# A decoder layer in fp32 pieces: a quarter of the projection of p moved ahead of the first product, with changes of order at the entries and the end

## The chip, the cores and the metric

The kernel runs on one core of a Trainium2 chip. The metric is the device time of one execution in microseconds (us). The engines are TensorE (PE, matmuls; its weight loads are shown as PEld), VectorE (DVE), ScalarE (ACT), GpSimd (POOL) and SyncE (SP). Nearly all transfers are issued on SP's queue, some on POOL's.

## The reference

One layer over 1024 tokens of width 1024, in fp32. Cut to what matters here:

```python
x = x + 0.5 * swiglu(rms_norm(x, ffn1_norm), ffn1_w_gate, ffn1_w_up, ffn1_w_down)   # D_FF = 2816
h = rms_norm(x, mix_norm)
fq, fk, fv, f_logit, sq, sk, sv, g_fox, g_sb = split_columns(h @ w_in)
...                          # forgetting attention (8 heads) and stick-breaking attention (8 heads)
x = x + (sigmoid(g_fox) * (y_fox @ w_branch_fox) + sigmoid(g_sb) * (y_sb @ w_branch_sb)) @ w_out
x = x + 0.5 * swiglu(rms_norm(x, ffn2_norm), ffn2_w_gate, ffn2_w_up, ffn2_w_down)
x = x + sigmoid(rms_norm(x, ple_norm) @ w_ple_gate) * (p @ w_ple_proj)      # p: 1024 x 256
```

The last product, p @ w_ple_proj, depends on the inputs alone, so it can be computed at any place. It is a matrix of 1024 features by 1024 tokens with an inner size of 256.

## The kernel before

All products are fp32 by splitting: an operand is cast to a "high" half (fp32r), the rest is its "low" half, and high*high, high*low and low*high are accumulated. Casts are on ACT, the subtractions for low halves on DVE or POOL (`split`, L105 and L106). Features lie on partitions; a PSUM bank holds 128 features by 512 tokens.

The stages follow one another: FFN 1 (its front is `first_entry`), the mixer's gates and projections, attention, the output projection, FFN 2, and the last stage (`ple_start`), which computes sigmoid(...) * (p @ w_ple_proj) and stores the output. The large products are done in pairs of 128-column weight blocks by seven products instead of eight, numbered 1 to 7 (`make_up`; L617 is the matmul). `up_order` is the list of products (n, m): n is the pair, m the product. It is the same for FFN 1, the mixer's gates, FFN 2 and the last stage; its first ten steps are called an entry here. Products 1, 6, 7 and 4 of one n share a PSUM bank ("b"); the result after 6 is copied out by ACT before 7 adds into that bank. `begin(s)` does operand sums that belong to step s of the list.

The order on each engine is that in which the code is written in these stages (a manual schedule). A few instructions outside them are placed by the scheduler; one is the scaling of the small tile `gqk` (q_norm and k_norm, L1615 to L1617), used only in attention.

In `first_entry` the eight token tiles of x are loaded (512 KB each, L1527) with the first weights between them, the norm's gain is spread over all partitions by two matmuls (`spread`, L239), `busy(4)` runs four matmuls on zeros (L253), tokens are squared and scaled, turned by PE (L273), and cast (`rows_high`, L282) and subtracted (`rows_low`, L287) into the operands H. The first product is `F.plain(0, 0, ...)` (L561).

In attention the projection of p is done in 16 units (`p_units`): group d of 512 features, four blocks m, two token halves, six matmuls of 128x512 each (L1056). Each result is copied from PSUM to a tile and stored in `p_proj` (DRAM). Around them stand the stacks of query and key of the first head, and behind them the first scores (L1150, L1151), which need the bias tile GF, loaded from `forget_sums` (L1430) and added to the mask by POOL (L1142).

In the last stage the list `AT` says behind which step the `p_proj` tiles are fetched and the results finished. `finish` multiplies a gate tile by `p_proj` on DVE (L1716) and adds `x_end`: by an accumulating DMA on POOL's queue (L1719) followed by the output store on the same queue (L1722), or, for the last pieces, by a DVE addition (L1721) and a store on SP's queue.

Of the kernel before, what the change touches and what calls it, by code (L numbers as in the profile page):

```python
# [11 lines left out]
F32R = mybir.dt.float32r  # L12
BF16 = mybir.dt.bfloat16
AF = mybir.ActivationFunctionType
ALU = mybir.AluOpType
# [3 lines left out]
P = 128  # L19
# [17 lines left out]
def tile_hybrid_decoder_layer(  # L37
# [42 lines left out]
    def pe(ins):  # L80
        order("pe", ins)
# [163 lines left out]
    def busy(n):  # L245

        if not zero:
            zero.append(slot("T", [P, 512], BF16))
            nc.vector.memset(zero[0][:], 0.0)
            return  # L250
        ps = bank("av")
        for _ in range(n):
            pe(nc.tensor.matmul(ps[:], zero[0][:, 0:P], zero[0][:], start=True, stop=True))  # L253

    def rows_stat(N, t, tag, first=False):
        xt = N["x"][:, t, :]
# [27 lines left out]
    def rows_low(N, t):  # L284
        cs = slice(t * P, (t + 1) * P)
        for b, v in enumerate(N["v"].pop(t)):
            nc.vector.tensor_sub(N["B"][b][:, 1, :, cs], v, f(N["B"][b][:, 0, :, cs]))  # L287
# [741 lines left out]
    def p_units(d, pT, new_bank):  # L1029

        cell = {}
        add_load(cell, lambda: wload([kp(w_ple_proj[0])[:, :, d * 512:d * 512 + 512]], 2, 512))

        def fetch():
            weights(cell, 1)
            for k in range(2):
                pT[k] = slot("RAW", [P, S])
                nc.sync.dma_start(pT[k][:], p[0, 0, k * P:(k + 1) * P, :])
            return
            yield  # L1040

        def operand(k):
            if k == 0:
                pT["t"] = slot("X", [P, 2, 2, S], F32R)
            split(pT["t"][:, k, 0, :], pT["t"][:, k, 1, :], pT[k][:], nc.scalar, nc.vector)
            return
            yield

        def unit(t):
            w = weights(cell)  # L1050
            ps = new_bank()
            m, half = divmod(t, 2)
# [6 lines left out]
            if half == 0:  # L1059
# [3 lines left out]
            if half:  # L1063
# [458 lines left out]
    def first_entry(F):  # L1522
# [30 lines left out]
        F.prep(0, 1)  # L1553
        rows_high(N[0], 2, ps2)
# [148 lines left out]
    def ple_start():  # L1703
# [9 lines left out]
        def finish(n, i, h=slice(0, 2), cols=slice(0, 512), add_in_dma=True):  # L1713

            e = E[n][i][:, h, cols]
            nc.vector.tensor_mul(e, e, T[n, i][:, h, cols])  # L1716
            queue = nc.gpsimd if add_in_dma else nc.sync
            if add_in_dma:
                queue.dma_start(e, xe[2 * n + i].rearrange("p (h n) -> p h n", h=2)[:, h, cols], accum_op=ALU.add)  # L1719
            else:  # L1720
                nc.vector.tensor_add(e, e, T[n, i, "x"][:, h, cols])  # L1721
            queue.dma_start(out[0, (2 * n + i) * P:(2 * n + i + 1) * P, :].rearrange("p (h n) -> p h n", h=2)[:, h, cols], e)  # L1722
# [4 lines left out]

        def evict(n, m, ps):
            if m == 1:
                E[n] = [slot(t, [P, 2, 512]) for t in (("Y", "Y") if n == 2 else ("GF", "RN"))]  # L1730
            e1, e2 = E[n]
            if m == 1:
                nc.scalar.copy(e1[:, 0, :], ps[:])
# [18 lines left out]
        AT = {4: [(finish, 0, 0)], 5: [(fetch, 2, 1, "T")], 6: [(finish, 0, 1), (fetch, 1, 0, "Q"), (fetch, 1, 1, "Q"), (fetch, 3, 0, "KH"), (fetch, 3, 0, "KH", True)],  # L1752
              7: [(fetch, 3, 1, "T")], 9: [(finish, 1, 0)], 10: [(fetch, 3, 1, "Q", True)], 11: [(finish, 1, 1)], 12: [(fetch, 2, 0, "Q")],
              13: [(finish, 2, 1)], 14: [(finish, 3, 0, h0), (fetch, 2, 0, "T", True)], 16: [(finish, 3, 1, h1, *late)], 17: [(finish, 2, 0, slice(0, 2), *late), (finish, 3, 0, h1, *late)]}

        def begin(i, X):
            if not Xs:
# [56 lines left out]
```

## Time and profile before

| what | value |
|---|---|
| median of 3 runs | 2258.56 us (2258.21 to 2259.16) |
| the profiled execution, its own time | 2257.49 us |
| its span in the trace | 2255.8 us |
| PE busy | 2213.0 us (98%) |
| DVE, ACT, POOL busy | 1507.5, 1005.5, 823.3 us |
| granted clock of PE | 0.996 of full speed |
| DMA | 298.30 MB, mean 132 GB/s over the span |

A timeline row gives the start, the busy time, the engine, the line, the operation with its output and input tiles, how many, and in brackets the idle time before it with what ended that idle time. "SPq" and "POOLq" rows are transfers being issued; their landing is later. A row of the stretches (A:B) gives the busy time of PE, PEld, DVE, ACT and POOL with counts, then the clock, the DMA share and GB/s. A row of the DMA view gives tile, queue, count, size and microseconds from issue to landing.

### The profile page before, as it was taken

Reading aid. Unit: us, or ns where it says so; the run is one execution under the profiler, and the core shown is the slowest. Engines: PE = TensorE matmul, PEld = TensorE weight load, DVE = VectorE, ACT = ScalarE, POOL = GpSimd, SP = SyncE. Lnnn points to the kernel's source line nnn. Section 1 sums busy time; section 2 is a strip of 40 time slices with the busy share of each in tenths; the row PEclk is TensorE's granted clock in tenths of the full one; section 3 lists DMA queues with packets and bytes.
Section 4 is the critical chain, followed back from the end, with each engine's and each line's share of the span. In section 5 each row is a group of like instructions: output and inputs, shape, how many; then the busy total and the mean of one; then the engine's idle time right before and its main releaser. Section 6 shows DMA issues by size and latency. Waiting matters only on the chain. (4 is left out here: it accounts for less than half of the span.)

```text
span 2255.8 us, 30537 instructions
## 1 busy us (share of the span) xinstructions
PE 2213.0 (98%) x11210; PEld 1879.2 (83%) x11210; DVE 1507.5 (67%) x2365; ACT 1005.5 (45%) x1805; POOL 823.3 (36%) x794
## 2 busy tenths in 40 slices
PE   9999999999999999999999999999999999999996
PEld 7788888888888899999898888888888888888885
DVE  8755555588887325666678775799554545778895
ACT  6333333433455445555566663255333333433452
POOL 2344535200021336565567664411544444100211
PEclk9999999999999999999999999999999999999998
DMA  3332323394323333333323366641323232754427
GB/s 131 103 126 82 129 80 131 126 332 173 112 94 123 120 115 103 85 113 85 85 66 93 104 196 233 244 159 45 127 103 108 95 116 94 281 196 149 140 84 210
DMA packets 196263, 298.30 MB, mean 132 GB/s; under 512 B 28745, under 2 KB 108873, under 8 KB 196114
## 3 DMA queue, kind: packets, MB, share of 16 engines
q1 hardware_dynamic: 194448, 290.58, 39.1%
q0 software_dynamic: 1664, 5.77, 1.1%
q8 instruction: 88, 1.44, 0.3%
q14 instruction: 61, 0.50, 0.1%
q10 hardware_dynamic: 2, 0.00, 0.0%
HBM read 196.40 MB, written 83.13 MB: 124 GB/s over the span
## 5 line engine op out<-in xcount | busy, mean ns | idle before, releaser
L509 PE MATMUL ps<-H,H 128*128 128x512 f32 x2184 | 497.3, 389 | 0.0
L509 PEld LDWEIGHTS ps<-H,H 128*128 128x128 f32 x2184 | 409.5, 188 | 84.9
L617 PE MATMUL ps<-H,WL 128*128 128x512 f32 x1164 | 275.5, 389 | 0.7 <-ACT GF L1735 0.7
L617 PEld LDWEIGHTS ps<-H,WL 128*128 128x128 f32 x1164 | 218.4, 188 | 46.4 <-ACT GF L1735 1.1
L185 POOL TENSOR_TENSOR PT<-PT,PT 128x512 f32<-128x512 f32 x27 | 35.0, 1294 | 403.9 <-ACT PT L182 403.0
L617 PE MATMUL ps<-H,Q 128*128 128x512 f32 x624 | 148.4, 389 | 0.0
L517 DVE SCALAR_TENSOR_TENSOR X<-ps,X 128x512 f32<-128x512 f32 x168 | 110.3, 686 | 47.4 <-PE ps L509 47.3
L617 PE MATMUL ps<-X,WL 128*128 128x512 f32 (+1 forms) x588 | 138.9, 385 | 1.1 <-ACT Y L779 0.7
L617 PEld LDWEIGHTS ps<-H,Q 128*128 128x128 f32 x624 | 117.1, 188 | 24.3
L617 PE MATMUL ps<-H,PT 128*128 128x512 f32 x540 | 128.8, 389 | 0.0
L617 PEld LDWEIGHTS ps<-X,WL 128*128 128x128 f32 x588 | 108.8, 188 | 23.8 <-ACT Y L779 1.1
L139 POOL TENSOR_TENSOR WL<-RAW,WH 128x512 fp32r<-128x512 f32 (+1 forms) x84 | 97.4, 1181 | 67.3 <-ACT WH L129 43.2
L1217 DVE TENSOR_TENSOR PT<-ps,PT 128x512 fp32r<-128x512 f32 (+1 forms) x160 | 100.0, 627 | 31.0 <-ACT PT L1211 30.1
L617 PEld LDWEIGHTS ps<-H,PT 128*128 128x128 f32 x540 | 101.2, 188 | 21.3 <-ACT GF L1735 0.3
L894 PE MATMUL ps<-WH,H 128*128 128x256 f32 x768 | 116.1, 287 | 0.8 <-ACT RN L959 0.8
L902 PE MATMUL ps<-H,WH 128*128 128x512 f32 x384 | 115.0, 406 | 0.0
L1235 PE MATMUL ps<-PT,X 128*128 128x256 f32 (+1 forms) x640 | 102.7, 286 | 6.5 <-DVE PT L1217 5.5
L1211 ACT CAST PT<-ps 128x512 fp32r<-128x512 f32 (+1 forms) x160 | 87.1, 548 | 42.6 <-PE ps L1209 41.5
L1235 PEld LDWEIGHTS ps<-PT,X 128*128 128x128 f32 x640 | 90.3, 190 | 17.2 <-DVE PT L1217 10.4
L894 PEld LDWEIGHTS ps<-WH,H 128*128 128x128 f32 x768 | 101.4, 190 | 2.6 <-ACT RN L959 1.2
L412 POOL TENSOR_TENSOR PT<-GF,RN 128x512 f32<-128x512 f32 x20 | 33.6, 1682 | 190.8 <-DVE GF L802 190.8
L1163 POOL TENSOR_TENSOR T<-T,l 128x128 f32<-128x128 f32 (+3 forms) x64 | 73.2, 1148 | 71.9 <-DVE l L1162 69.7
(441 smaller groups left out, 4781.7 us busy)
## 6 DMA issues: line engine op xcount, KB each, us to landing
hidden<-PT SPq DMA_DIRECT2D x40, 512.0 KB, 2.6
WH<-in_ffn_w_gate_dram SPq DMA_DIRECT2D x38, 512.0 KB, 4.7
Q<-hidden SPq DMA_DIRECT2D x24, 512.0 KB, 6.0
hidden<-RN SPq DMA_DIRECT2D x22, 512.0 KB, 2.6
KH<-in_ffn_w_up_dram SPq DMA_DIRECT2D x20, 512.0 KB, 6.2
KL<-in_ffn_w_up_dram SPq DMA_DIRECT2D x20, 512.0 KB, 6.9
T<-in_ffn_w_down_dram SPq DMA_DIRECT2D x20, 512.0 KB, 6.5
GF<-hidden SPq DMA_DIRECT2D x14, 512.0 KB, 7.7
```

The costliest lines, as they stand in the source:

```text
L139: ins = eng_lo.tensor_sub(lo[part], raw[part], f(hi[part]))
L185: add = lambda eng: eng.tensor_add(N["acc"], N["acc"], d)
L412: eng.tensor_add(s12[:, 0, :], g1[:, 1, :], g2[:, 1, :])
L509: pe(nc.tensor.matmul(groups[g][t][:], wt[:, b, k, t * P:(t + 1) * P], act[:, a, k, :], start=(fresh and n == 0), stop=(i in (6, 1, 4) and ...
L517: nc.vector.scalar_tensor_tensor(xs, groups[g][t][:], scale, xs, ALU.mult, ALU.add)
L617: pe(nc.tensor.matmul(ps[:, cols], hl[:, a, k, :], right(B[m], b, k)[:, cols], start=(first and i == 0), stop=(final and i == 11), skip_gr ...
L894: pe(nc.tensor.matmul(ps[:, :n], hT[t // 4](a, k)[:, (t % 4) * P:(t % 4 + 1) * P], w[k // 4][b][:, k % 4, :n], start=(i == 0), stop=(i == ...
L902: pe(nc.tensor.matmul(ps[:], w[a][:, k, :], hT[half](b, k), start=(i == 0), stop=(i == 23)))
L1163: nc.gpsimd.tensor_mul(T[:, :n], T[:, :n], l[:].broadcast_to([P, n]))
L1211: high = nc.scalar.copy(pt[:, 0, :width], ps[:, :width])
L1217: ins = nc.vector.tensor_sub(pt[:, 1, :width], ps[:, :width], f(pt[:, 0, :width]))
L1235: pe(nc.tensor.matmul(o, lh, r, start=(kpair == c and i == 0), stop=(kpair == 0 and i == 3)))
```

## The change

- In the front, `p_begin` loads the first 512 tokens of p and the first 512 columns of w_ple_proj ahead of x. `p_split` makes their halves. Four products (`p_product`) of 128 features by 512 tokens stand between the turnings of the token tiles, and `p_out` copies and stores them. In attention, group 0 keeps only the second token half (four units instead of eight); it still loads and splits all of p.
- `busy(4)` goes, and `busy(6)` stands ahead of the spreading of the gain.
- In `up_order`, (2, 6) and (1, 7) change places; in `begin`, the operands of product 7 are made in step 1 instead of step 0.
- In the last stage all output stores go to SP's queue, the stores of accumulated tiles as separate steps (`store`), the half tile (3, 0) is finished by a DVE addition, and fetches, finishes and tiles are placed anew (`AT`).

The diff, cut to its core:

```diff
+    def p_begin():
+        raw = slot("Q", [P, 2, 512])
+        nc.sync.dma_start(raw[:], kp(p[0, 0])[:, :, 0:512])
+        wr = slot("RAW", [P, 2, 512])
+        nc.sync.dma_start(wr[:], kp(w_ple_proj[0])[:, :, 0:512])
+        return raw, wr
+    def p_split(raw, wr):
+        r = []
+        for src, tags in ((raw, ("KH", "KL")), (wr, ("RN", "GF"))):
+            hi, lo = (slot(t, [P, 2, 512], F32R) for t in tags)
+            split(hi[:], lo[:], src[:], nc.scalar, nc.vector)
+            r.append((hi, lo))
+        return r
+    def p_product(ops, m, ps):
+        n = 0
+        for a, b in ((0, 0), (1, 0), (0, 1)):
+            for k in range(2):
+                pe(nc.tensor.matmul(ps[:], ops[1][b][:, k, m * P:(m + 1) * P], ops[0][a][:, k, :], start=(n == 0), stop=(n == 5)))
+                n += 1
+        return ps
+    def p_out(m, ps):
+        o = slot("T", [P, 512])
+        nc.scalar.copy(o[:], ps[:])
+        nc.sync.dma_start(pd[m][:, 0:512], o[:])
...
-        seqn = [(2, 1), (1, 5), (2, 2), (1, 6), (1, 7), (2, 6), (2, 5), (1, 3), (2, 7), (1, 4)]
+        seqn = [(2, 1), (1, 5), (2, 2), (1, 6), (2, 6), (1, 7), (2, 5), (1, 3), (2, 7), (1, 4)]
...
             if s == 0:
                 sums(2, nc.vector, True)
+            elif s == 1:
                 for q in range(4):
                     combo_s(q, 7)
...
-        units = [(6 * 0.216, unit(t)) for t in range(NT)]
+        units = [(6 * 0.216, unit(t)) for t in range(d == 0, NT, 1 + (d == 0))]
...
+        p_raw = p_begin()
         load_x(0)
...
         busy(0)
+        busy(6)
         spread(N[0]["g"])
...
+        p_ops = p_split(*p_raw)
         for t in range(4):
             rows_stat(N[0], t, ("PT", "WL", "WL", "PT")[t], True)
             rows_mul(N[0], t)
-        busy(4)
+        pu = [p_product(p_ops, m, bank("sc")) for m in range(2)]
+        p_out(0, pu[0])
         rows_high(N[0], 0, ps1)
+        p_out(1, pu[1])
+        pu.append(p_product(p_ops, 2, bank("sc")))
         rows_high(N[0], 1, ps1)
...
         rows_low(N[0], 2)
+        p_out(3, p_product(p_ops, 3, ps2()))
...
-            queue = nc.gpsimd if add_in_dma else nc.sync
             if add_in_dma:
-                queue.dma_start(e, xe[...], accum_op=ALU.add)
+                nc.gpsimd.dma_start(e, xe[...], accum_op=ALU.add)
             else:
                 nc.vector.tensor_add(e, e, T[n, i, "x"][:, h, cols])
-            queue.dma_start(out[...], e)
+                store(n, i, h, cols)
+        def store(n, i, h=slice(0, 2), cols=slice(0, 512)):
+            nc.sync.dma_start(out[...], E[n][i][:, h, cols])
...
-        AT = {4: [(finish, 0, 0)], 5: [(fetch, 2, 1, "T")], 6: [(finish, 0, 1), ...
+        AT = {6: [(fetch, 1, 0, "Q"), (fetch, 1, 1, "WH")], 7: [(finish, 0, 0)], 8: [(finish, 0, 1), ...
```

What this does to the order on the engines, at three places. The names of semaphores in brackets say which engine or which transfer lane an instruction waits for.

VectorE in the front, from the low halves of token tile 0 (ps to H) on. WL is the low half of the first weight block. Before:

```order
L287 TENSOR_TENSOR H_106<-ps_169,H_106 128x4x128 [waits Activation_49]
L287 TENSOR_TENSOR H_107<-ps_174,H_107 128x4x128 [waits Activation_49]
L106 TENSOR_TENSOR WL_195<-WH_121,WL_195 128x512 [waits DMAHW5_49,Activation_49]
L287 TENSOR_TENSOR H_106<-ps_181,H_106 128x4x128 [waits PE_49]
L287 TENSOR_TENSOR H_107<-ps_186,H_107 128x4x128 [waits PE_49]
L287 TENSOR_TENSOR H_106<-ps_198,H_106 128x4x128 [waits Activation_49]
```

Now:

```order
L316 TENSOR_TENSOR H_110<-ps_200,H_110 128x4x128 [waits Activation_49]
L316 TENSOR_TENSOR H_111<-ps_205,H_111 128x4x128 [waits Activation_49]
L1657 TENSOR_SCALAR gqk<-gqk 64x1 [waits DMAHW2_49]
L106 TENSOR_TENSOR WL_236<-WH_132,WL_236 128x512 [waits DMAHW7_49,Activation_49]
L316 TENSOR_TENSOR H_110<-ps_222,H_110 128x4x128 [waits PE_49]
L316 TENSOR_TENSOR H_111<-ps_227,H_111 128x4x128 [waits PE_49]
L316 TENSOR_TENSOR H_110<-ps_242,H_110 128x4x128 [waits Activation_49]
```

The scaling of gqk, which waits for the load of q_norm, has moved here; before it stood some 20 instructions further on.

TensorE in the front, now, from the turning of the last token tile (identf) to the first product (H_110 with WL_236). KH and KL are the halves of p, RN and GF those of its weights:

```order
L302 MATMUL ps_261<-identf,PT_176 128x128 x3
L275 MATMUL ps_270<-KH_147,RN_151 128x512 [waits DVE_49]
L275 MATMUL ps_270<-KH_147,RN_151 128x512
L275 MATMUL ps_270<-KL_148,RN_151 128x512 x2
L275 MATMUL ps_270<-KH_147,GF_152 128x512 x2
L590 MATMUL ps_297<-H_110,WL_236 128x512 [waits Activation_49]
L590 MATMUL ps_297<-H_110,WL_236 128x512 x7
```

The fourth product of p stands directly ahead of the first product. Its bank is the one that ps_242 had, so it waits for VectorE to have taken the low half from that (the last row of the fence above). Before, the first product followed the turning.

GpSimd's queue in the last stage. GF, RN and Y hold the gate tiles, x_end the residual. Before:

```order
L1719 DMA GF_18851<-x_end 128x1024 [waits DMAHW4_49,DMAHW5_49,DMAHW0_49,DMAHW6_49,DVE_49,Activation_49]
L1722 DMA out_dram<-GF_18851 128x1024 [waits DMASW0_49]
L1719 DMA RN_18852<-x_end 128x1024 [waits DMAHW5_49,DMAHW1_49,DMAHW7_49,DVE_49,Activation_49]
L1722 DMA out_dram<-RN_18852 128x1024 [waits DMASW2_49]
L585 TENSOR_TENSOR WH_19129<-WH_19129,KL_19242 128x4x128 [waits DMAHW2_49,DMAHW3_49,DMAHW1_49,DVE_49]
```

Now, on the same queue:

```order
L1758 DMA GF_18873<-x_end 128x1024 [waits DMAHW3_49,DMAHW4_49,DMAHW2_49,DMAHW6_49,DVE_49,Activation_49]
L614 TENSOR_TENSOR WH_19151<-WH_19151,KL_19252 128x4x128 [waits DMAHW1_49,DMAHW7_49,DMAHW0_49,DVE_49]
L1758 DMA RN_18874<-x_end 128x1024 [waits DMAHW5_49,DMAHW3_49,DVE_49]
L1758 DMA GF_18953<-x_end 128x1024 [waits DMAHW3_49,DMAHW0_49,DVE_49]
L1758 DMA RN_18954<-x_end 128x1024 [waits DVE_49,Activation_49]
L1758 DMA Y_19078<-x_end 128x1024 [waits DMAHW0_49,DMAHW4_49,DVE_49,Activation_49]
```

And on SyncE's queue now, to its end:

```order
L1764 DMA out_dram<-GF_18873 128x1024 [waits DMAHW0_49,DMASW0_49]
L1764 DMA out_dram<-RN_18874 128x1024 [waits DMAHW1_49,DMASW1_49]
L1751 DMA GF_19345<-x_end 128x1024 [waits DMAHW0_49]
L1751 DMA RAW_19365<-p_proj 128x1024 [waits DMAHW3_49]
L1751 DMA RAW_19367<-x_end 128x1024 [waits DMAHW4_49,DVE_49]
L1764 DMA out_dram<-KH_19297 128x512 [waits DMAHW5_49,DVE_49]
L1764 DMA out_dram<-GF_18953 128x1024 [waits DMAHW6_49,DMASW2_49]
L1764 DMA out_dram<-RN_18954 128x1024 [waits DMAHW7_49,DMASW3_49]
L1764 DMA out_dram<-KH_19298 128x512 [waits DVE_49,Activation_49]
L1764 DMA out_dram<-Y_19078 128x1024 [waits DMAHW1_49,DMASW4_49]
L1764 DMA out_dram<-Y_19077 128x1024 [waits DMAHW2_49,DVE_49]
L1764 DMA out_dram<-KH_19297 128x512 [waits DMAHW3_49,DVE_49]
```

The stores, each waiting for its accumulation (DMASW), have gone from POOL's queue to SP's, with two fetches of x_end and one of p_proj between them.

More of the change, by code (lines that the diff above doesn't have):

```diff
@@ L1058, in unit @@
                     yield 0.216
-            if half == 0:
+            if half == 0 or d == 0:
                 cell["o"] = slot("PT", [P, 2, 512])
@@ L1062, in unit @@
             nc.scalar.copy(o[:, half, :], ps[:])
-            if half:
+            if d == 0:
+                nc.sync.dma_start(pd[m][:, 512:], o[:, 1, :])
+            elif half:
                 nc.sync.dma_start(pd[4 * d + m], o[:].rearrange("p h n -> p (h n)"))
-        units = [(6 * 0.216, unit(t)) for t in range(NT)]
+        units = [(6 * 0.216, unit(t)) for t in range(d == 0, NT, 1 + (d == 0))]
         return [(0.0, fetch())] + [(0.0, operand(k)) for k in range(2)] + units if d == 0 else units
@@ L1553, in first_entry @@
         F.prep(0, 1)
+        p_out(2, pu[2])
         rows_high(N[0], 2, ps2)
@@ L1716, in finish @@
             nc.vector.tensor_mul(e, e, T[n, i][:, h, cols])
-            queue = nc.gpsimd if add_in_dma else nc.sync
             if add_in_dma:
-                queue.dma_start(e, xe[2 * n + i].rearrange("p (h n) -> p h n", h=2)[:, h, cols], accum_op=ALU.add)
+                nc.gpsimd.dma_start(e, xe[2 * n + i].rearrange("p (h n) -> p h n", h=2)[:, h, cols], accum_op=ALU.add)
             else:
                 nc.vector.tensor_add(e, e, T[n, i, "x"][:, h, cols])
-            queue.dma_start(out[0, (2 * n + i) * P:(2 * n + i + 1) * P, :].rearrange("p (h n) -> p h n", h=2)[:, h, cols], e)
+                store(n, i, h, cols)
+        def store(n, i, h=slice(0, 2), cols=slice(0, 512)):
+            nc.sync.dma_start(out[0, (2 * n + i) * P:(2 * n + i + 1) * P, :].rearrange("p (h n) -> p h n", h=2)[:, h, cols], E[n][i][:, h, cols])
         F = make_up(N, lambda n: kp(w_ple_gate[0])[:, :, n * 256:n * 256 + 256], 4, tags_p, AF.Sigmoid)
@@ L1729, in evict @@
             if m == 1:
-                E[n] = [slot(t, [P, 2, 512]) for t in (("Y", "Y") if n == 2 else ("GF", "RN"))]
+                E[n] = [slot(t, [P, 2, 512]) for t in ({2: ("Y", "Y"), 3: ("KH", "KH")}.get(n, ("GF", "RN")))]
             e1, e2 = E[n]
@@ L1751, in ple_start @@
         late = (slice(0, 512), False)
-        AT = {4: [(finish, 0, 0)], 5: [(fetch, 2, 1, "T")], 6: [(finish, 0, 1), (fetch, 1, 0, "Q"), (fetch, 1, 1, "Q"), (fetch, 3, 0, "KH"), (fetch, 3, 0, "KH", True)],
-              7: [(fetch, 3, 1, "T")], 9: [(finish, 1, 0)], 10: [(fetch, 3, 1, "Q", True)], 11: [(finish, 1, 1)], 12: [(fetch, 2, 0, "Q")],
-              13: [(finish, 2, 1)], 14: [(finish, 3, 0, h0), (fetch, 2, 0, "T", True)], 16: [(finish, 3, 1, h1, *late)], 17: [(finish, 2, 0, slice(0, 2), *late), (finish, 3, 0, h1, *late)]}
+        AT = {6: [(fetch, 1, 0, "Q"), (fetch, 1, 1, "WH")], 7: [(finish, 0, 0)], 8: [(finish, 0, 1), (fetch, 3, 0, "Q", True), (fetch, 2, 1, "T")],
+              9: [(fetch, 3, 0, "T")], 10: [(finish, 1, 0)], 11: [(finish, 1, 1), (fetch, 3, 1, "Q"), (store, 0, 0)], 12: [(store, 0, 1), (fetch, 3, 1, "GF", True)],
+              13: [(finish, 2, 1), (fetch, 2, 0, "RAW"), (fetch, 2, 0, "RAW", True)], 14: [(finish, 3, 0, h0, *late), (store, 1, 0)], 15: [(store, 1, 1)],
+              16: [(finish, 3, 1, h1, *late)], 17: [(store, 2, 1), (finish, 2, 0, slice(0, 2), *late), (finish, 3, 0, h1, *late)]}
         def begin(i, X):
```

## The prediction

> **What bounds the kernel now.** I read the page first, then the timeline of the last 60 us, of the first 30 us, of TensorE's gaps over the whole span, and of the start of attention.
>
> ```profile
> span 2255.8 us, 30537 instructions
> PE 2213.0 (98%) x11210; PEld 1879.2 (83%) x11210; DVE 1507.5 (67%) x2365; ACT 1005.5 (45%) x1805; POOL 823.3 (36%) x794
> ```
>
> TensorE (PE) is busy for all but 42.8 us. So what a change is worth is almost entirely what it does to those 42.8 us, plus the matmuls it takes off a stretch where TensorE never stops. The largest single gap is the end:
>
> ```profile
> 2234.70 1.69 PE L617 MATMUL ps<-X,WL 128*128 128x256 f32 x12 [0.47 <-ACT RN L1775]
> 2238.11 1.12 SPq L1722 DMA_DIRECT2D out_dram<-RN  x2
> 2239.46 0.58 POOL L1722 DMA_DIRECT2D out_dram<-RN  x1 [6.29 <-DMA RN<-x_end]
> 2240.17 0.87 POOL L1719 DMA_DIRECT2D Y<-x_end  x1
> 2246.63 0.56 POOL L1722 DMA_DIRECT2D out_dram<-Y  x1 [5.59 <-DMA Y<-x_end]
> 2247.27 0.88 POOL L1719 DMA_DIRECT2D GF<-x_end  x1
> 2252.29 0.57 POOL L1722 DMA_DIRECT2D out_dram<-GF  x1 [4.14 <-DMA GF<-x_end]
> ```
>
> TensorE ends at 2236.4 and SyncE (SP) has issued its last output store at 2239.2, yet the span lasts to 2255.8. What runs there is GpSimd's queue (POOL): it adds x_end to a tile by an accumulating DMA, waits until that has landed, issues the store of it, and only then the next accumulation. The kernel ends on that chain: the last store is asked for at 2252.29, lands 2.3 us later, and the span ends 1.2 us after that.
>
> **Part 1, the end.** The change puts every output store into SP's queue and turns the sixth accumulation (GF, half a tile) into a vector add. POOL then issues five accumulations and waits for none.
>
> ```profile
> out_dram<-GF POOLq DMA_DIRECT2D x1, 256.0 KB, 2.3
> out_dram<-RN SPq DMA_DIRECT2D x2, 128.0 KB, 3.1
> T<-p_proj SPq DMA_DIRECT2D x4, 512.0 KB, 5.8
> Y<-x_end POOLq DMA_DIRECT2D x1, 512.0 KB, 6.1
> DMA to landing us min/median/max: 4.7/7.3/9.7
> 2213.60 0.89 POOL L1719 DMA_DIRECT2D RN<-x_end  x1
> 2225.44 1.22 DVE L1716 TENSOR_TENSOR Y<-Y,T 128x1024 f32<-128x1024 f32 x1
> 2231.44 0.69 DVE L1721 TENSOR_TENSOR RN<-RN,Q 128x512 f32<-128x512 f32 x1
> 2234.69 1.23 DVE L1721 TENSOR_TENSOR Y<-Y,T 128x1024 f32<-128x1024 f32 x1
> ```
>
> The last arithmetic, on VectorE, stays as it is, so SP's last store (128 KB) is issued as now, from 2238.9 on. It lands 2.3 us later if the queues are as empty as for POOL's last store, 3.1 if not, and 1.2 us later the span ends: 2242.4 to 2243.2. I take the first: a gain of 13.4 us, with 12.6 at the other end; far less if the five accumulations do not overlap (a rival below).
>
> Two things on SP could spoil this, since each of its stores waits for its accumulation with all later ones behind it. The fifth accumulation (Y) follows the multiply that ends at 2226.7; at 7.3 us (the row of least, median and most for all six at L1719) it lands at 2234.0, before SP could issue the next store, whose data VectorE finishes at 2235.9. And the fetch of x_end into GF now stands behind the stores of the first two accumulated tiles. The second accumulation goes out at about 2213.6 as now and lands by 2221 to 2223; a fetch then takes about 5.8, to 2229, and VectorE wants it at 2231.4.
>
> The Trainium skill, "DMA: Bandwidth & Descriptors", section "Issuing engines are not separate DMA queues", says that spreading DMAs over issuing engines saves only issue time. By that rule the end would save the six POOL store issues, about 0.57 us each, 3.4 us instead of 13.4, and the sum below would be +2.7 us. The rows above disagree here: POOL's time goes into waits of 4.14 to 6.29 us between issues, not into the issues.
>
> **Part 2, attention.** Twenty-four matmuls of 128x512 leave.
>
> ```profile
> 1530.27 5.44 PE ps L617 x24
> 825.00:848.00 23.00, 23.00 (x108) 18.93 (x106) 1.50 (x2) 11.85 (x20) 7.94 (x10) 1.00 0.74 234
> 838.83 0.42 SPq L1430 DMA_DIRECT2D GF<-forget_sums  x1
> 844.88 2.56 POOL L1142 TENSOR_TENSOR T<-GF,mask_fox 128x128 f32<-128x128 f32 x6 [4.32 <-DMA GF<-forget_sums]
> 847.98 0.22 PE L1150 MATMUL ps<-KH,Q 128*128 128x128 f32 x1
> 848.47 0.29 DVE L1155 CUSTOM_DVE_ANT_0 T<-T,ps 128x128 f32<-128x128 f32 x1 [15.14 <-PE ps L1151]
> ```
>
> Twenty-four such matmuls take 5.44 us, and TensorE is busy for all of the 23 us in which the projection runs, so 5.44 us is the most that can be won. But the first scores would then start at 842.5, and the first vector step on them needs the bias tile, which lands at 844.88 now. Its load stays behind the same number of projection stores on SP after the query stack; without one weight cast ahead of a copy it may go 0.9 us earlier. With one mask addition (2.56/6 = 0.43) behind the landing, the first vector step can start at 844.5 to 845.3, 3.2 to 4.0 us earlier than 848.47. I take 3.5 us, with 2.0 and 5.4 as bounds.
>
> **Part 3, the entries.** TensorE's other gaps, found window by window:
>
> ```profile
> 59.37 3.01 PE L617 MATMUL ps<-X,WL 128*128 128x512 f32 x12 [0.67 <-ACT Y L779]
> 76.14 2.11 PE L617 MATMUL ps<-X,Q 128*128 128x512 f32 x8 [1.97 <-DVE X L653]
> 696.48 1.20 PE L617 MATMUL ps<-T,WL 128*128 128x512 f32 x4 [0.68 <-ACT GF L1316]
> 1558.15 2.11 PE L617 MATMUL ps<-T,WL 128*128 128x512 f32 x8 [0.68 <-ACT Y L779]
> 2192.99 3.01 PE L617 MATMUL ps<-H,WL 128*128 128x512 f32 x12 [0.68 <-ACT GF L1735]
> 2208.17 2.35 PE L617 MATMUL ps<-X,PT 128*128 128x512 f32 x9 [0.60 <-ACT X L649]
> 25.00:76.00 51.00, 48.49 (x221) 39.63 (x219) 48.92 (x82) 28.69 (x56) 0.45 (x1) 1.00 0.14 43
> ```
>
> In each of the four entries product (1,7) adds into the bank that the copy after (1,6) is still reading, and waits 0.67 to 0.68 us. With (2,6) between them the copy has a product's time (2.72 us) to finish. That is 2.0 us for the second to fourth entry. The wait of 0.60 in the last entry stands behind two vector multiplies of the output that now come later: 0.4 (0 to 0.6). In the first entry VectorE is busy 48.92 of 51 us and TensorE waits for it at 76.14, so the 0.67 there only lengthens the 1.97: I count 0, between a gain of 2.6 and a loss of 0.6 (a vector step that now waits for its cast).
>
> **Part 4, the front.** Added: two loads of 512 KB ahead of x, two casts on ScalarE, two subtractions on VectorE, 24 matmuls, four copies, four stores of 256 KB. What decides is the order on VectorE. The scaling of gqk (L1617) ran at 29.28, long after its load had landed; now it stands between the low halves of token tile 0 and everything else of VectorE.
>
> ```profile
> 7.72 1.89 PE L253 MATMUL ps<-T 128*128 128x512 bf16 x4
> 14.48 0.57 SPq L1615 DMA_DIRECT2D gqk<-in_q_norm_dram  x1
> 14.80 0.69 DVE L106 TENSOR_TENSOR WL<-WH,WL 128x512 fp32r<-128x512 f32 x1
> 15.41 3.67 DVE L287 TENSOR_TENSOR H<-ps,H 128x512 fp32r<-128x512 f32 x6
> 16.28 6.19 PE L561 MATMUL ps<-H,WL 128*128 128x512 f32 x24 [0.86 <-ACT H L282]
> 18.54 3.50 PEld L561 LDWEIGHTS ps<-H,WL 128*128 128x128 f32 x16 [0.57 <-DVE H L287]
> 29.28 0.14 DVE L1617 TENSOR_SCALAR gqk<-gqk 64x1 f32<-64x1 f32 x1
> gqk<-in_q_norm_dram SPq DMA_DIRECT2D x1, 0.2 KB, 6.2
> 8.00:16.30 8.30, 7.09 (x37) 5.55 (x35) 8.09 (x10) 6.59 (x15) 2.59 (x3) 1.00 1.05 391
> ```
>
> Now the load of q_norm is issued at 14.48 and lands 6.2 us later, at 20.7, because 4 MB of x and 2 MB of weights go ahead of it at 391 GB/s. The change puts 1.05 MB more ahead: 1.05/0.391 = 2.7 us, landing at 23.4. VectorE, which did the step ahead of it at about 14 and meets x 2.7 us later, reaches the scaling at about 16 to 17 and stands until 23.4. Then follow 0.14 for it, 0.69 for the weight's low half, and three subtractions at 0.61 (3.67/6) up to the one that frees the PSUM bank of the fourth projection product: 26.1. That product of six matmuls stands ahead of the first product in TensorE's order. At 0.227 us each (5.44/24) it ends at 27.5; at the 0.47 of L253 (1.89/4), the nearest row of matmuls after idle time, at 28.9. TensorE will have stood idle for some 8 us, so I take 28.9. Against 16.28 that is +12.6; the 0.57 that the first product now waits for low halves is covered: +12.0 us. The lower end is 10.6 (27.5), the upper 14, if the first eight matmuls of the first product run at 0.47 too. The two casts, two subtractions, four copies and the first three projection products lie ahead of or under that stall and cost nothing beyond it; q_norm's wait hides them. The six matmuls on zeros, now ahead of the spreading of the gain, run while TensorE waits for that gain anyway.
>
> The Trainium skill, "TensorE: Matmul & The Clock Gate", section "Part 1: The HAM clock gate", says that an idle window of about 3.4 us halves the clock until about 3.4 us of activity have passed. By that rule some eight matmuls run slow, which fits the value taken; the trace agrees as far as it goes (0.47 us for a matmul in L253, 0.227 later).
>
> Without that stall x still comes 2.7 us later and the fourth projection product (1.36) still stands ahead of the first product: +4 us, the price of the front if the wait is not there.
>
> **Sum.** -13.4 - 3.5 - 2.0 - 0.4 + 0 + 12.0 = -7.3 us. The profiled execution took 2257.49 (span 2255.8); the median of the runs, 2258.56, is 1.07 above it. On the profile that gives 2250.2, on the median 2251.3.
>
> **Rivals.**
>
> A: the front costs little. If q_norm lands by 17, VectorE never stands and the front costs +4. Then -15.3: 2243.3. Against it speaks the saturated window of 391 GB/s; for it, only that a load of 0.2 KB needs no bandwidth itself. Chance 0.10.
>
> B, slower: the accumulations follow one another in POOL's queue although POOL no longer waits. They start at about 2209; five at the longest landing, 9.7, end at 2257.5, and SP's store of the fifth with four more stores behind it (0.34 each) and a landing of 3.1 ends the span at 2262.3, 6.5 later than now instead of 13.4 earlier. Sum +12.6: 2271.2. At the median of 7.3 the span would end at 2250.3, a gain of 5.5 and a sum of +0.6. It makes the kernel slower by more than can be told from no change from about 8.1 us each on. Against it: the shortest, of 256 KB, takes 4.7 us and one of 512 KB takes 6.1, so much of each is fixed time that can overlap. Chance 0.07. This is also how the rule of the Trainium skill on issuing engines (the page named in part 1) would come true here.
>
> C: about no change. The end gains only 8 to 10 us, because the late fetch of x_end into GF, now behind two stores that wait for accumulations, reaches VectorE late, and attention gains 2. Sum -0.4 to -2.4: 2256.2 to 2258.2. For it: fetches, stores and accumulations all run at once between 2221 and 2229. Against it: about 3 us of slack in each. Chance 0.13.
>
> Forecast: 0.70.
>
> **The numbers.** The runs differ by 0.95 us in 2258.56, and 0.2% (4.5 us) is about what a measurement of this kernel can tell from no change. The forecast's own bounds (front 10.6 to 14, first entry -2.6 to +0.6, other entries 2.6 to 2.0, attention 5.4 to 2.0, end 13.4 to 12.6) sum to -13.4 and -2.0, so 2245.2 to 2256.6. The range reaches a little past them, to 2244.0 and 2257.0, takes in part of C and of A, and leaves out B and the rest of both, 0.2 in all. Faster by more than 0.2% (below 2254.0): 0.79; within: 0.14; slower: 0.07.
>
> **What would show it.** Right: the scaling of gqk on VectorE starts at 23 to 24 after an idle time of 6 us or more on the DMA of q_norm; the fourth projection product starts near 26 and the first product near 28; the bias tile's landing and not TensorE sets the first vector step of attention; the 0.68 waits are gone from the last three entries; the span ends within 6 us of the last matmul, with no POOL instruction in it. Wrong: the first product starts by 21 (A); POOL or SP waits for an accumulation after the last matmul (B); VectorE waits for GF<-x_end after 2230 (C).

## The result, and the profile after

The changed kernel takes 2258.32 us (median of 12 runs, 2255.83 to 2259.93) beside 2259.70 for the kernel before on the same chip: a ratio of 0.9994 with a 95% interval of 0.9985 to 1.0003. A second set gave 2258.02 beside 2258.82, 0.9995 (0.9986 to 1.0004). That is no difference that can be told; 2251.3 was forecast, and the result lies above the range. The profiled execution took 2259.11, its span 2257.4:

```profile
span 2257.4 us, 30554 instructions
PE 2217.1 (98%) x11212; PEld 1882.7 (83%) x11212; DVE 1512.1 (67%) x2368; ACT 1007.6 (45%) x1807; POOL 819.1 (36%) x787
```

To see where the time goes I follow one TensorE instruction at four places: the first up product of FFN 1 (the first one with the up weights), a product behind its entry, the first matmul of the forget sums, and the first up product of the last stage. The timeline of before:

```profile
31.24 5.70 PE L617 MATMUL ps<-H,PT 128*128 128x512 f32 x24
80.81 2.88 PE L617 MATMUL ps<-X,PT 128*128 128x512 f32 x12
821.81 0.38 PE L1103 MATMUL ps<-GF,log_f 128*8 128x128 f32 x2
2181.28 2.88 PE L617 MATMUL ps<-H,PT 128*128 128x512 f32 x12
```

The same four after:

```profile
44.33 5.73 PE L646 MATMUL ps<-H,PT 128*128 128x512 f32 x24
95.10 2.88 PE L646 MATMUL ps<-X,PT 128*128 128x512 f32 x12
835.91 0.39 PE L1135 MATMUL ps<-GF,log_f 128*8 128x128 f32 x2
2191.23 2.88 PE L646 MATMUL ps<-H,PT 128*128 128x512 f32 x12
```

| stretch | forecast | measured |
|---|---|---|
| front, to the first up product | +12.0 | 44.33 - 31.24 = +13.1 |
| first entry | 0 | 14.3 - 13.1 = +1.2 |
| to the forget sums (mixer's entry) | -0.7 | 14.1 - 14.3 = -0.2 |
| to the last stage (attention, FFN 2's entry) | -4.2 | 9.95 - 14.1 = -4.1 |
| last stage, to the end of the span | -14.5 | 66.2 - 74.5 = -8.3 |
| sum | -7.4 (-7.3 but for rounding) | +1.7 (spans: +1.6) |

The front went as described. In its timeline and stretches the scaling of gqk stands where the scheduler put it, TensorE waits 8.15 us, and the granted clock (the third figure from the end) is half:

```profile
23.14 0.15 DVE L1657 TENSOR_SCALAR gqk<-gqk 64x1 f32<-64x1 f32 x1 [6.47 <-DMA gqk<-in_q_norm_dram]
25.77 1.22 PE L275 MATMUL ps<-KH,RN 128*128 128x512 f32 x2 [8.15 <-DVE H L316]
28.49 7.07 PE L590 MATMUL ps<-H,WL 128*128 128x512 f32 x24
28.00:30.00 2.00, 2.00 (x6) 1.55 (x5) 0.00 (x0) 1.27 (x2) 0.00 (x0) 0.50 0.00 0
```

In attention the size came as forecast: the first vector step on scores is 859.31 - 848.47 = 10.8 late after 14.1, a gain of 3.3. It waits for the mask addition (`POOL T L1174`), as described. But ahead of that addition on GpSimd now stands a weight subtraction (L139) that waited for ScalarE's cast, and the addition follows it without a pause:

```profile
857.56 1.28 POOL L139 TENSOR_TENSOR WL<-RAW,WH 128x512 fp32r<-128x512 f32 x1 [8.83 <-ACT WH L129]
858.83 1.28 POOL L1174 TENSOR_TENSOR T<-GF,mask_fox 128x128 f32<-128x128 f32 x3
859.31 0.29 DVE L1187 CUSTOM_DVE_ANT_0 T<-T,ps 128x128 f32<-128x128 f32 x1 [11.36 <-POOL T L1174]
```

In the entries the 0.67 to 0.68 waits on the copy are gone, but each has another in its place:

```profile
82.48 4.61 PE L646 MATMUL ps<-T,WL 128*128 128x512 f32 x12 [2.51 <-DVE Y L812]
718.73 3.01 PE L646 MATMUL ps<-H,WL 128*128 128x512 f32 x12 [0.47 <-DVE RN L1351]
1576.26 3.02 PE L646 MATMUL ps<-H,WL 128*128 128x512 f32 x12 [0.53 <-DVE Y L812]
2210.91 5.78 PE L646 MATMUL ps<-H,WL 128*128 128x512 f32 x24 [0.48 <-DVE RN L1780]
```

These are product (1,3). It adds into the bank that the vector addition behind (1,7) still reads (L812, L1351, L1780), and with (1,7) one place later only (2,5) lies between them, not (2,6) and (2,5).

The end of the last stage, SP's queue, then VectorE and TensorE:

```profile
2227.37 0.94 SPq L1764 DMA_DIRECT2D out_dram<-GF  x1
2232.22 0.34 SPq L1764 DMA_DIRECT2D out_dram<-RN  x1
2239.90 0.33 SPq L1751 DMA_DIRECT2D GF<-x_end  x1
2251.42 1.96 SPq L1764 DMA_DIRECT2D out_dram<-KH  x3
2245.36 0.69 DVE L1760 TENSOR_TENSOR KH<-KH,GF 128x512 f32<-128x512 f32 x1 [5.58 <-DMA GF<-x_end]
2247.64 2.93 PE L646 MATMUL ps<-X,WL 128*128 128x256 f32 x12 [5.04 <-ACT KH L1818]
```

GpSimd's chain is gone, and the span ends 6.8 us behind the last matmul instead of 19.4 (within 6 was forecast). But the last matmul ends 14.2 later than before (2250.57, not 2236.39). This looks like rival C to the letter: the fetch into GF waits on SP until the store of GF has landed (7.3 us), VectorE waits 5.58 for it, and TensorE's last half product 5.04. The experiments say otherwise.

### The profile page after: what moved, and what is told of

Read it like the earlier page. It is cut to its first block, busy times and chain, and to the rows that moved or that the text cites. A ratio compares the mean times of both kernels' runs of the same rounds, so it can differ in the third digit from the quotient of the medians.

```text
span 2257.4 us, 30554 instructions
## 1 busy us (share of the span) xinstructions
PE 2217.1 (98%) x11212; PEld 1882.7 (83%) x11212; DVE 1512.1 (67%) x2368; ACT 1007.6 (45%) x1807; POOL 819.1 (36%) x787
## 3 DMA queue, kind: packets, MB, share of 16 engines
q0 software_dynamic: 720, 2.62, 0.6%
## 4 chain that ended last, share of the span: by engine, by line
PE 84%; DVE 9%; ACT 2%; DMA 2%; issue 1%; POOL 0%; SPq 0%; ACTq 0%; DVEq 0%; POOLq 0%
PE ps L646 36%; PE ps L538 22%; PE ps L924 7%; PE ps L932 5%; PE ps L1529 4%; PE ps L1267 3%; PE ps L1241 2%; PE ps L590 1%; PE ps L1183 1%; PE ps L1182 1%; DVE PT L1249 1%; DVE WL L106 1%; PE ps L1086 1%; DVE RN L1145 1%; DMA out_dram<-GF 1%
## 5 line engine op out<-in xcount | busy, mean ns | idle before, releaser
L139 POOL TENSOR_TENSOR WL<-RAW,WH 128x512 fp32r<-128x512 f32 (+1 forms) x84 | 98.5, 1194 | 69.2 <-ACT WH L129 44.6
```

The lines of the kernel that those rows point to most:

```text
L139: ins = eng_lo.tensor_sub(lo[part], raw[part], f(hi[part]))
```

## The experiments

Each was timed beside the kernel before on the same chip. "Last stage" is the time from its first up product (H,PT x12 near 2181) to the end of the span.

**The three parts alone.** The last stage alone (`finish`, `store`, tiles, `AT` of the diff on the kernel before):

> The kernel before with only the change of the last stage (stores on SP, half tile by a vector add, fetches placed anew). Theory 1 (the tail gains 12.6 behind the last matmul and gives 5.8 back in the wait for GF<-x_end and the slow last half product): 6 to 7.5 us faster than before. Theory 2 (the tail was as good as its sum and the loss lies in the front and the entries): 12.5 us or more faster.

2248.71 beside 2259.09, 0.9952 (0.9939 to 0.9964); last stage 64.1. So it is worth 10.4 us, between the two theories (6 to 7.5, 12.5 or more), though the late fetch is in it.

The move of p alone (the diff without `up_order`, `begin` and the last stage):

> The kernel before with only the move of the quarter of the projection of p (front and attention), old orders, old last stage. Theory 1 (by the shifts in the two traces: first product over 13.1 us late, attention gives back 4.0): 9 to 10 us slower than before, 2268 to 2269.5. The prediction's own terms, +12.0 and -3.5: 8.5 slower. Theory 2 (the front is cheap by itself and the loss is made together with the new orders): under 5 us slower.

2267.18 beside 2259.37, 1.0036 (1.0023 to 1.0049): 7.8 slower. In its trace the first up product is 13.0 late and the last stage 9.4, so attention returns 3.6.

The orders alone:

> The kernel before with only the new order of the entries ((2,6) ahead of (1,7), operands of product 7 one step later), nothing else. The prediction's terms: 2.0 to 2.4 us faster, the first entry unchanged. Theory 1 (product (1,3) now waits for the vector addition behind the copy of (1,7), 0.47 to 0.53 in three entries, and 2.5 us in the first, where VectorE is behind): within 1 us of before, either side; in the first entry a wait of 2 us or more on Y before product (1,3).

2258.57 beside 2259.37, 0.9997 (0.9988 to 1.0006): 0.8, no difference that can be told. The waits on the vector addition are all there: 2.50 in the first entry, then 0.47, 0.51 and, in the last one, 1.60. The parts add up to -3.4; together they gave -0.8 to -1.4, within what the intervals leave.

**The front's wait.**

```diff
-    nc.vector.tensor_scalar(gqk[0:HD, :], ...)     # placed by the scheduler
+        F.sums(1, nc.vector)
+        nc.vector.tensor_scalar(gqk[0:HD, :], ...)  # in first_entry, loads behind the gains
```

> The changed kernel with one edit: the scaling of gqk stands on VectorE behind the operand sums of the second weight pair instead of ahead of the first product. Theory 1 (the front's price is that wait): VectorE goes on at 16.7, six subtractions and a cast's remainder later the fourth projection product and the first product start at 20.6 to 22 instead of 28.5, TensorE keeps its full clock, and the end of the first product moves from 35.4 to 27 to 28; the kernel gains 7 to 8.5 us, 2250 to 2251.5. Theory 2 (the added 1 MB of loads and the four copies hold the front as well): the first product still starts at 25 or later and the gain is below 3.5 us.

2252.42, 0.9970 (0.9958 to 0.9982), 6 us under the changed kernel, a little less than theory 1's 7 to 8.5 and well above theory 2's 3.5. The six executions lie between 2248.99 and 2253.91; the one in the trace took 2249.28, so its front is one of the better ones:

```profile
19.33 0.73 PE L275 MATMUL ps<-KH,RN 128*128 128x512 f32 x2 [1.52 <-DVE H L316]
20.82 5.63 PE L590 MATMUL ps<-H,WL 128*128 128x512 f32 x24
```

The first product starts 7.7 earlier than in the changed kernel and at full clock, as theory 1 had it; the first up product is then 4.05 behind the kernel before.

**The late fetch.**

```diff
-  11: [..., (fetch, 3, 1, "Q"), (store, 0, 0)], 12: [(store, 0, 1), (fetch, 3, 1, "GF", True)]
+  11: [..., (fetch, 3, 1, "KL", True), (fetch, 3, 1, "Q"), (store, 0, 0)], 12: [(store, 0, 1)]
```

> The changed kernel with one edit: the late fetch of x_end for the last half tile goes into a free KL slot, ahead of the first output store in SP's queue, instead of into GF behind two stores. Theory 1 (that fetch held VectorE, ScalarE and then TensorE's last half product): it is issued at about 2224 and lands by 2233, VectorE's wait of 5.58 and TensorE's of 5.04 are gone, the last half product keeps its full clock (1.7 instead of 2.93), and the span ends 5 to 6 us earlier, 2252.5 to 2253.5. Theory 2 (the DMA engines are full from 2220 on, share 0.98 to 1.05, and set the end whatever the order of the queue): the wait goes, but the last stores land as late as now; gain under 2 us.

2256.45, 0.9989 (0.9980 to 0.9998), 1.6 to 1.9 us under the changed kernel, as theory 2 had it; last stage 64.0 instead of 66.2 in the first and 64.6 in the second profile of the changed kernel. TensorE's wait is down to 0.47 and its last half product back at full clock, but VectorE now waits for the next tile, issued at 2232.47 and landed 12 us later:

```profile
2242.18 1.69 PE L646 MATMUL ps<-X,WL 128*128 128x256 f32 x12 [0.47 <-ACT KH L1818]
2244.45 1.23 DVE L1756 TENSOR_TENSOR Y<-Y,RAW 128x1024 f32<-128x1024 f32 x1 [3.45 <-DMA RAW<-p_proj]
```

Both edits together:

> Both edits together: the scaling of gqk late, and the fetch of x_end into KL ahead of the stores. Theory 1: the two are far apart and add up, 12 to 14 us under the changed kernel, 2244.5 to 2246.5. Theory 2: below 5.5 us together.

2251.32, 0.9963 (0.9951 to 0.9976): 7 us under the changed kernel, between the theories (12 to 14, and below 5.5). Theory 1 fails at the end.

The new last stage with the orders and without the move of p, fetch early and fetch late:

> The kernel before with the new last stage, the new orders and the early fetch of x_end into KL, but without the move of the projection of p. Theory 1: the tail gives about 10.4 as in the run with the tail alone, the early fetch 1.5 to 3 more, the orders about 0: 2245.5 to 2248. If the move of p with a late scaling of gqk costs nothing net (front +4, attention -4), this equals the run with both edits, 2251.3, within 2 us; if it lies 3 us or more under it, the move loses time even without the wait for q_norm.

> The kernel before with the new last stage and the new orders, x_end fetched late into GF as in the changed kernel, no move of p. From the start of the last stage's second product group to the end of the span, the run with the tail alone took 64.1 us, the one with the early fetch 64.1, the changed kernel 66.2. Theory late fetch (with the new orders it costs 1.5 to 2 us, whatever the DMA engines do): 65.5 to 66.2 here, 1.5 to 2 us slower than the run with the early fetch. Theory saturation (the DMA engines set the end, the order of the queue costs nothing): 64 to 64.5, within 1 us of it.

2247.84, 0.9949 (0.9935 to 0.9963), and 2248.00, 0.9950 (0.9938 to 0.9963); last stage 64.1 and 64.5. The late fetch, with a wait of 4.50 of TensorE behind it, costs 0.2 us of the median, 0.7 if each is taken against the kernel before beside it. The two runs also put a price on the move of p without its wait, 2251.32 against 2247.84: it loses 3.5 us.

**What sets the end.** All remaining fetches ahead of the stores:

```diff
-  12: [(store, 0, 1)], 13: [(finish, 2, 1), (fetch, 2, 0, "RAW"), (fetch, 2, 0, "RAW", True)]
+  11: [..., (fetch, 2, 0, "RAW"), (store, 0, 0)], 12: [(fetch, 2, 0, "RAW", True), (store, 0, 1)], 13: [(finish, 2, 1)]
```

> The run without the move of p (new last stage, new orders, x_end into KL), and in addition all remaining fetches ahead of the output stores they stood behind: p_proj and x_end of tile (2,0) go into RAW before the stores of (0,0) and (0,1). Theory order (a fetch is late because a store stands ahead of it in SP's queue): VectorE's wait of about 3 us for RAW goes and the end comes 2 to 3 us earlier, 2245 to 2246. Theory saturation (the 16 DMA engines are full from 2213 to 2243 at about 270 GB/s while accumulations run): bytes and engine time stay the same, so the stores are late instead; under 1 us.

2247.84 again (0.9953, 0.9941 to 0.9966): nothing. VectorE's last step does end 1.2 us earlier, counted from the start of the stage, but the last two stores then take 4.8 us to land instead of 3.5. And on top of it one accumulation turned into a load and a vector add:

> The same with one of the five accumulating DMAs replaced: x_end of tile (2,1) is loaded into a free KL slot and added on VectorE (1.23 us more for it). Theory saturation: an accumulating DMA costs 5.2 us of all engines per MB (2.62 MB, 29.8% of 46 us) and a plain one 2.7 (7.34 MB, 43.2%), so 0.52 MB saves 1.3 us of the full stretch, and the span ends 1 to 1.5 us earlier than in the run with the fetches ahead. Theory order: no gain from it, 0 to 1 us later since VectorE has 1.23 us more behind the last products.

2247.83 (0.9950, 0.9938 to 0.9963), last stage 64.0. Its trace has new waits on both engines, and the end does not move:

```profile
2232.60 1.22 DVE L1728 TENSOR_TENSOR Y<-Y,KL 128x1024 f32<-128x1024 f32 x1 [5.59 <-DMA KL<-x_end]
2237.34 2.93 PE L617 MATMUL ps<-X,WL 128*128 128x256 f32 x12 [4.80 <-ACT KH L1786]
```

The 1.3 us that saturation promised did not show. The engine time is saved, as the last 8 us of the run with the fetches ahead and of this one show (busy share of the DMA engines 0.81 and 0.64, the figure before the last). But VectorE, held until 2232.60, is late with the data of the last stores (its last step ends at 2241.65 instead of 2239.45):

```profile
2236.80:2244.80 8.00, 0.00 (x0) 0.00 (x0) 2.54 (x6) 0.00 (x0) 0.00 (x0) 0.60 0.81 323
2237.19:2245.19 8.00, 2.93 (x12) 2.63 (x12) 4.33 (x8) 0.47 (x2) 0.00 (x0) 0.50 0.64 249
```

So I took the price of accumulating away at the same bytes and order. This kernel leaves the gated projection out of five tiles and serves for the time alone:

```diff
-  nc.gpsimd.dma_start(e, xe[...], accum_op=ALU.add)
+  nc.gpsimd.dma_start(e, xe[...])
```

> The run without the move of p and with the early fetch, in which the five transfers of x_end on GpSimd's queue write instead of accumulate (their tiles then hold x_end alone, without the gated projection). Same bytes, same order. Theory saturation (an accumulating transfer takes the DMA engines 5.2 us per MB, a plain one 2.7): 2.62 MB save 6.5 us of full engines; the wait for RAW is gone, the end is set by the last product and vector steps, 4 to 6 us earlier. Theory order: the queue is the same, so the end is within 1 us.

2242.29 beside 2258.82, 0.9925 (0.9912 to 0.9939): 5.0 to 5.5 us under the same kernel with accumulation, last stage 59.2 instead of 64.1. The stretches of the last 32 and 24 us (the last two figures are the busy share of the DMA engines and GB/s), and GpSimd's DMA queue from 2200 on (packets, MB, share of 16 engines). With accumulation:

```profile
2213.33:2221.33 8.00, 8.00 (x37) 6.60 (x37) 6.71 (x8) 3.10 (x7) 3.99 (x4) 1.00 0.98 236
2221.33:2229.33 8.00, 8.00 (x37) 6.64 (x36) 5.21 (x8) 2.02 (x5) 0.89 (x1) 1.00 1.05 277
2229.33:2237.33 8.00, 5.00 (x33) 4.28 (x31) 3.42 (x5) 2.39 (x4) 0.00 (x0) 1.00 1.04 343
2237.33:2245.33 8.00, 0.00 (x0) 0.00 (x0) 3.72 (x7) 0.00 (x0) 0.00 (x0) 0.59 0.76 301
q0 software_dynamic: 720, 2.62, 23.7%
```

Without:

```profile
2213.12:2221.12 8.00, 8.00 (x37) 6.60 (x37) 6.73 (x8) 3.10 (x7) 3.03 (x4) 1.00 0.88 269
2221.12:2229.12 8.00, 8.00 (x37) 6.64 (x36) 5.19 (x8) 2.02 (x5) 0.54 (x1) 1.00 1.02 418
2229.12:2237.12 8.00, 5.01 (x33) 4.30 (x31) 7.07 (x11) 2.40 (x4) 0.00 (x0) 1.00 1.03 414
q0 software_dynamic: 720, 2.62, 12.5%
```

From 2213 on the engines are full in the first and, but for the first stretch (0.88), in the second. The same 720 packets of 2.62 MB take 23.7% of the engines when they accumulate and 12.5% when they only write, 1.9 times as much, and while they run the 16 engines move 277 GB/s instead of 418. 11.2% of 58 us is 6.5 us, of which 4.9 reach the end. That accumulating costs these 4.9 us is shown. That it does so by filling the DMA engines rests on the shares near 1 and on the run with the fetches ahead, where another order changed nothing. The plain transfers also land sooner, so SP waits less for them (not at all for Y, instead of 2.9 us); no run takes that apart from the engine time.

The changed kernel repeated beside these two:

> The changed kernel once more, beside the other two. All theories: 2257 to 2259.5; the part of the last stage 65 to 66.2 us by theory late fetch, 64 to 65 with the rest from its front by theory saturation.

Last stage 64.6. The 66.2 of the first profile was in part that execution's.

**The entries, and a better kernel.** In the list, (2,7) ahead of (1,3), on top of both edits:

> The changed kernel with both edits (scaling of gqk late, x_end into KL) and in the list of products (2,7) ahead of (1,3), so that two products lie between (1,7) and (1,3). Theory 1: the waits of 0.46 to 0.48 on the vector addition go in the later entries, and in the first entry 2.6 us of idle time and the slow clock behind it (1.5 us) shrink, since the addition has 2.72 us more: 2 to 5 us under the run with both edits. Theory 2 (VectorE sets the pace of the first entry, so its next operand is late instead): the wait moves to the following product and only about 1 us is won.

2248.89, 0.9954 (0.9941 to 0.9966), 2.4 under the run with both edits. No wait is left in the three later entries. In the first entry VectorE is behind, and the wait goes to the next operand, at the half clock again:

```profile
81.72 4.60 PE L646 MATMUL ps<-X,Q 128*128 128x512 f32 x12 [3.21 <-ACT X L678]
```

So the old list for the first entry and this one for the others, with the plain add and without the move of p; then the same with it:

> The same, with the orders mended: the old list in the first entry, and in the three later ones (2,6) between (1,6) and (1,7) and (2,5), (2,7) between (1,7) and (1,3). No move of p. The waits of 0.68 and of 0.46 to 0.51 are both gone in the later entries (about 1.4 us), the first entry waits 2.6 in all as before instead of 3.4 to 4.5: 1.5 to 3 us faster than the run with the plain add, 2242 to 2244.

> The same again, with the move of p and the scaling of gqk behind the operand sums. The front costs 4 to 6 (first up product 35.3 to 37.3 instead of 31.2), attention gives 3.6 back: 0.5 to 2.5 us slower than the run without the move. If the move had been worth making with its one wait removed, it would be 1 us or more faster instead.

2244.69 beside 2258.57, 0.9939 (0.9927 to 0.9952), and 2248.28, 0.9947 (0.9933 to 0.9961). The first beats both kernels, by 13.9 and about 13 us, and the run with the plain add by 3.1. The move of p costs 3.6 here, more than the 0.5 to 2.5 expected, but the five executions with it lie between 2243.52 and 2250.91 (2244.32 to 2246.31 without), and the one in the trace is the slowest. In the two traces the first up product comes at 39.40 instead of 31.08, 8.3 late, and the last stage is still 7.3 late. Attention returns 2.7 up to its first vector step, but only 1.0 in all: behind a wait of 1.6 us on the first scores the granted clock falls to 0.83 in this execution. The stretch there, first with the move, then without:

```profile
850.00:870.00 20.00, 17.77 (x112) 16.73 (x112) 9.34 (x44) 8.77 (x23) 11.38 (x16) 0.83 0.53 160
842.00:862.00 20.00, 19.70 (x135) 18.08 (x134) 9.40 (x43) 10.91 (x27) 11.39 (x16) 1.00 0.68 211
```

## Why the prediction was wrong

On the profile the result lies 9 us above the forecast. Of that, 6.2 us are in the last stage (4.5 in the second profile of the changed kernel), 1.1 in the front, 1.2 in the first entry, and most of the rest in the other entries.

**Front** (+12.0, measured +13.1). Right: the wait for q_norm, the fourth projection product at 25.8, the first product at 28.5 and at half the clock. The bound of 14 was the nearer end. The run with the scaling put late shows the mechanism. The +4 that the prediction gave the front without that wait was 4.05 in that run, 6 to 8 in three others, so this smaller price was sized too low.

**Attention** (-3.5, measured -3.3 at the first vector step, -3.6 in the run with the move alone). The size is right, the reason only in part, so the agreement is partly luck. The prediction let the mask addition start as soon as the bias tile lands. In the changed kernel the tile, issued at 852.38, lands 6.1 to 6.4 us later, just when GpSimd ends its weight subtraction at 858.8, so the two can't be told apart. In the run with the move alone the tile has landed 0.8 to 1.0 us before the addition starts, and GpSimd's order sets it. In the four runs without the front's wait the addition waits 0.4 to 0.6 us for the tile, as described, and the gain up to the first vector step is 2.7 to 2.8.

**First entry** (0, measured +1.2). The forecast counted the wait that went, and allowed 0.6 for one that comes. What came is 2.51 of idle time, and 12 matmuls in 4.61 instead of 2.88.

**Other entries** (-2.0 and -0.4; the orders alone gave -0.8 in all). Wrong step: "With (2,6) between them the copy has a product's time (2.72 us) to finish". It has. But taking a product out from between (1,7) and (1,3) makes the next wait: the vector addition behind (1,7) reads the bank of products 5 and 3 ("d"), to which (1,3) adds, and I looked at the bank "b" alone.

**End** (-13.4; -10.4 alone). The failing step is "The last arithmetic, on VectorE, stays as it is, so SP's last store (128 KB) is issued as now, from 2238.9 on", with a landing "if the queues are as empty as for POOL's last store". In the run with the last stage alone VectorE ends at 2241.93 instead of 2238.83, and the last stores take 3.4 us to land instead of 2.3; in the changed kernel VectorE ends at 2252.98.

The queues were empty in that row because the chain on GpSimd's queue had spread the transfers out (DMA share 0.44 from 2245 to 2253). Asked for together they fill the engines, so loads land after 12 us instead of 5.8, and VectorE's last steps, not only the stores, come late. I had the row that could have warned, accumulations landing after 4.7 to 9.7 us, and read it as a latency that overlaps; 2.7 us of each 512 KB are time of all 16 engines (23.7% of 58 us for 2.62 MB). Without that price the forecast of this stage would have come out about right: the run with plain transfers and the early fetch takes 59.2 us for it, beside the 60.0 that the forecast adds up to (74.5 - 14.5).

A second error hides in the fetch of x_end into GF. The prediction had it issued right behind the stores and landed by 2229, 2.4 us before VectorE wants it. But it waits until the store of GF has landed, 12.5 us behind that store's issue (2227.37 and 2239.90 above). The runs with the fetch put early show that this is worth little. Also, the -0.4 and one of the 0.68 in the last entry were added to the end's gain: with the engines setting the end they are worth nothing that shows (last stage 64.1 with the old orders, 64.1 and 64.5 with the new).

**Rivals.** C gave 2256.2 to 2258.2 and named a late fetch into GF; the number was nearly right, the cause was not: without the late fetch the end gains 0.2 to 0.7 us in the kernel without the move of p, and under 2 in the changed one. A is out. B had the accumulations in each other's way in GpSimd's queue, and that is half right. In the run with the early fetch SP's stores of four of them go out at 2223.64, 2227.50, 2231.30 and 2235.11, each directly behind a landing: one accumulation lands every 3.8 us, not every 7.3 to 9.7, and the kernel did not become slower. The engines are full meanwhile, and the runs do not tell a turn in the queue from a share of the engines. (B's two times for the end also leave out the 1.2 us between the last landing and the end of the span that part 1 counts; no chance hangs on it.) Of the Trainium skill's page "DMA: Bandwidth & Descriptors", section "Issuing engines are not separate DMA queues", the first half holds here: all DMAs run on the same 16 engines and interleave, which is the 0.98 to 1.05 above. What it says of the saving, issue time alone, does not: the last stage alone, in which GpSimd no longer waits between its transfers, gained 10.4 us, not 3.4.

Whether the remaining 2 us between the parts' sum and the whole are real stays open.

## What to carry to other kernels

A chain of waits that is taken apart packs its transfers together: before counting its length as gain, add up the engine time of what will then run at once, an accumulating transfer at about twice a plain one (1.9 times here). Where the DMA engines are full, a wait in the trace shows only whose turn was last; removing it moves it to the next tile. The last stage took 64.0 to 64.5 us in six kernels that queue its transfers differently; over all kernels with the new last stage and accumulations it was 61.9 to 66.2, the shortest two with one accumulation fewer and the mended orders. And a step moved by one place in a list takes a gap from another pair: go through every bank that the list shares.

## What was not expected of the hardware

A pause of TensorE of 1.6 to 2.6 us sometimes lowers the granted clock and sometimes does not. Behind 2.51 us on the same product, 12 matmuls took 4.61 us in the changed kernel (granted clock 0.63 from 82.48 to 87.10) and 3.04 in the run without the move of p and with the early fetch:

```profile
69.30 3.04 PE L617 MATMUL ps<-T,WL 128*128 128x512 f32 x12 [2.51 <-DVE Y L783]
```

The Trainium skill's page "TensorE: Matmul & The Clock Gate" warns, in "Part 1: The HAM clock gate", of an idle window of about 3.4 us; here 2.51 us was enough in some executions. The wait of 1.6 us in attention, shown above at a clock of 0.83, left the clock whole in the run with both edits, where it was 1.5:

```profile
850.00:870.00 20.00, 17.08 (x125) 15.57 (x124) 12.03 (x52) 11.07 (x28) 12.99 (x18) 1.00 0.53 165
```

The fronts with the wait for q_norm removed differ too: the first product started at 20.8, 22.6, 22.8 and 24.5 us in four kernels whose code is the same up to there. What makes the difference was not followed.
